# A hybrid layer's attention heads: the samples' scores, log sums and outputs in one PSUM bank, cached keys loaded alone, weights split in quarters, last key tiles in free conv tiles

## The chip, the core and the metric

The kernel runs on one core of a Trainium2 chip. The metric is device time of one execution in microseconds (us): the median of three runs. The engines of the core have short names in the profile: PE is TensorE (matmuls and transposes), PEld its weight loads, ACT ScalarE, DVE VectorE, POOL GpSimd, and SP SyncE, which here only issues DMAs. PSUM, the memory that matmuls write, has eight banks of 512 float columns for each of 128 partitions.

## The reference

One layer of an encoder trunk is computed for 512 prompt frames and 64 sample frames (576 rows, `T`), with a model width of 2048. The 64 sample frames also attend to 512 cached frames.

```python
def stick_breaking(q, k, v, q_pos, k_pos):
    z = jnp.einsum('bqhd,bkhd->bhqk', q, k) / math.sqrt(HEAD_DIM)
    mask = (k_pos[None, :] < q_pos[:, None])[None, None]
    log_1mb = jnp.where(mask, jax.nn.log_sigmoid(-z), 0.0)
    after = lax.cumsum(log_1mb, axis=3, reverse=True) - log_1mb
    w = jnp.where(mask, jnp.exp(jax.nn.log_sigmoid(z) + after), 0.0)
    return jnp.einsum('bhqk,bkhd->bqhd', w, v)

def hybrid_layer(...):
    hn = rmsnorm(x, g_norm1)
    proj = hn @ w_in
    q, k, v, gb, gc, hc = jnp.split(proj, [...], axis=-1)
    ...
    o_attn = stick_breaking_blocks(q, k_all, v_all, P).reshape(B, T, ATTN_W)
    ...
    mix = jnp.concatenate([rmsnorm(o_attn, g_attn_out), rmsnorm(o_conv, g_conv_out)], axis=-1)
    x = x + mix @ w_out
    h2 = rmsnorm(x, g_norm2)
    x = x + (jax.nn.silu(h2 @ w_gate) * (h2 @ w_up)) @ w_down
    return x, k, v, new_conv
```

q and k are normalized per head (8 heads of 128), and `o_conv` is a short gated convolution over gb, gc and hc. New key and value rows and the convolution's state are outputs too.

## The kernel before

All products are made in float32 precision from two fp32r parts of each operand, a rounded high part and the rest: three matmuls (high by high, low by high, high by low) stand for one. ScalarE casts the high part and VectorE subtracts it. Activations lie channel by channel on the partitions with the 576 rows as columns, in two halves of 288 (`HALVES`).

*The input product* (about 0 to 603 us) runs over 22 units of two 128-column groups, each in seven products as in Strassen's scheme. `order` (L898 to L904) lists the pairs (unit, product) in the order in which TensorE runs them; unit -1 is the last, a pair of value heads, and unit -2 the last pair of query and key groups. For a product `run` issues 24 matmuls of 288 columns, and `prepare` four places ahead builds its weight form. `a_done` (L802 on) takes the sums out of PSUM: for values and for queries and keys into tiles `E`, allocated by `e_tile`, which have the tag "e" with two buffers. `normed` normalizes them 17 ticks later and stores them in `qk_dram` (L788); `tokens` transposes the key and value tiles (L749, L758) and stores the rows. For the convolution, tiles `c0` and `c1` of the pool `lpool` are used, whose last conv unit is gb 3 (n = -3). After the product (-1, 3), `xpool` is released and the eight groups of the convolution's result, `mixc`, are loaded from DRAM into its place (L920).

*The first half of the output projection* (603 to 817 us) multiplies `mixc` with eight blocks of 256 columns of w_out (`out_proj`, L978). Each block makes four sums `pjo` (three PSUM banks of the pool `ps_pj`), and each sum takes eight ticks of three matmuls (`product`, L214), 32 ticks for a block. VectorE scales a sum and adds it to the residual tiles `x2t` (L986, L987), which are loaded at the start (L969).

The eight heads run between these ticks. `Pipeline` calls generators when their tick has come: `yield 8` in `attend` means eight ticks later. A new head starts every 29 ticks (`PERIOD`). For TensorE, the order in which the program is written is the order of execution; on ACT, DVE, POOL and SP a scheduler decides it within the dependencies, and each of these queues then runs strictly in order. DMAs take eight semaphores in turn, so that a DMA's issue also waits until the one eight places before it has landed.

In `attend(h)`, the three PSUM banks z2, z1, z0 hold the prompt's scores (L1060), their softplus goes to ScalarE, VectorE and GpSimd, triangular matmuls add the log sums, `weights` (L1116) makes the exponentials, and `po` (L1152 on) sums the outputs. The samples have a path of their own: scores `zs` of 64 queries against four cached key blocks and the new one (L1085 to L1088), log sums `cz` (L1105 to L1109), exponentials in `ws` (L1114), outputs `os` (L1167 to L1170). `keys_cached` transposes the loaded cached keys `cK` on TensorE into `kc` and copies them to `kcT`; it is called eight ticks after zs for the next head (L1102). `kc`, `zs`, `cz`, `po` and `os` all come from `misc`, a tag with two banks used in turn. `load_qk` (L943) loads queries, keys and cached keys of the next head after zs, `load_v` its values at the end of the head. `mixed` (L1145) takes po and os out into the tiles `mixa`, and their squares go through the tiles `sqa` (L1164, L1165, L1172).

The samples' matmuls run on 128 query columns: the last 128 of the rows, of which the last 64 are the samples. The five blocks overlap in the bank at 64-column steps, each overwriting the useless half of the one before.

`next_weight` (L198) hands out the blocks of w_out and the first blocks of the gate and up weights, 20 in all, each 2048 wide per partition. At the start of block i it splits the whole of block i + 1 (two casts and two subtractions of 1024, L179 and L180), and loads block i + 2 (L187).

*The second half of the projection*, on `mixa` (to 917 us), and then the gate, up and down products follow.

Of the kernel before, what the change touches and what calls it, by code (L numbers as in the profile page):

```python
# [10 lines left out]
F32 = mybir.dt.float32  # L11
F32R = mybir.dt.float32r
AF = mybir.ActivationFunctionType
# [3 lines left out]
P = 128  # L17
# [84 lines left out]
def tile_hybrid_stream_step(  # L102
# [95 lines left out]
    def next_weight():  # L198
        i = pos[0]
        pos[0] += 1  # L200
        end = first_block
        while len(raws) < min(i + 2, end):
            load_weight()
        while len(ready) < min(i + 2, end):
            split_weight(nc.vector)
        while len(raws) < min(i + 3, end):
            load_weight()
        out = ready[i]
        ready[i] = None
        return out  # L210
# [591 lines left out]
    def a_done(n, c, i, ps, part):  # L802
        kind, g = UNITS[n][:2]
        a, b = HALVES[i]
        if kind in ("v", "qk"):
            if (n, c) not in etile:
                etile[n, c] = e_tile(f"E{n}")
            E = etile[n, c]
            bank = ps
            if part is not None:  # L810
                nc.vector.tensor_tensor(out=E[:, a:b], in0=ps, in1=part, op=ALU.add)  # L811
# [89 lines left out]
    for n in range(2 - NA, -3):  # L901
        order += [(n + 1, 1), (n, 3), (n, 4), (n + 1, 2), (n + 1, 6), (n + 1, 7), (n + 1, 5)]
    order += [(-2, 1), (-3, 3), (-3, 4), (-2, 2), (-2, 6), (-2, 5), (-2, 3), (-1, 1), (-1, 2), (-1, 3),
              (-2, 7), (-2, 4), (-1, 6), (-1, 5), (-1, 7), (-1, 4)]  # L904
# [25 lines left out]
    ws = bpool.tile([P, 384], F32, name="ws")  # L930
# [12 lines left out]
    def load_qk(h):  # L943
        nc.sync.dma_start(out=qf, in_=qk_dram[h, 0])
        nc.sync.dma_start(out=kf, in_=qk_dram[h, 1])
        nc.sync.dma_start(out=cK, in_=ck[:, h, :].rearrange("(i p) d -> p i d", p=P))
        split(qh, ql, qf[:, :TP])
        split(kh, kl, kf[:, :TP])

    load_qk(0)  # L950
    nc.vector.tensor_scalar(out=neg1r, in0=ident, scalar1=0.0, scalar2=-1.0, op0=ALU.mult, op1=ALU.add)
# [88 lines left out]
    def keys_cached():  # L1040
        kc = misc("kc")
        for i in range(4):
            nc.tensor.transpose(kc[:, i * P : (i + 1) * P], cK[:, i, :], ident)
        nc.scalar.copy(out=kcT, in_=kc)

# [3 lines left out]
    def attend(h):  # L1049
# [12 lines left out]
        for b in (2, 1, 0):  # L1062
# [19 lines left out]
            if h == 0 and b == 1:  # L1082
                keys_cached()

        zs = misc("zs")  # L1085
        for b in (4, 3, 2, 1, 0):
            lk = kf[:, T - P : T] if b == 4 else kcT[:, b * P : (b + 1) * P]
            mm(zs[:, b * TS : b * TS + P], lk, qf[:, T - P : T], start=True, stop=True, skip_group_check=True)  # L1088
        nc.scalar.copy(out=ws[:, TS:], in_=zs[:, TS : TS + 320])
        if h + 1 < NH:  # L1090
            load_qk(h + 1)
        softplus(sp[:, :320], ws[:, TS:], sp[:, :320])
# [8 lines left out]
        if h + 1 < NH:  # L1101
            keys_cached()  # L1102

        def sample_weights():
            cz = misc("cz")  # L1105
            mm(cz[:, :320], trir, sph[:, :320], start=True, stop=False, skip_group_check=True)
            mm(cz[:, :320], trir, spl[:, :320], stop=False, **kw)
            mm(cz[:, :256], neg1r, sph[:, 320:], stop=False, **kw)
            mm(cz[:, :256], neg1r, spl[:, 320:], stop=True, **kw)  # L1109
            nc.gpsimd.memset(ws[:, :TS], 0.0)  # L1110
            nc.vector.tensor_tensor(out=ws[:, TS:], in0=cz[:, :320], in1=ws[:, TS:], op=ALU.add)
# [40 lines left out]
        po = misc("po")  # L1152
# [14 lines left out]
        os_ = misc("os")  # L1167
        for b in range(5):
            lv = vtok[:, 4, :] if b == 4 else cV[:, b, :]
            mm(os_[:, :P], lv, ws[:, b * TS : b * TS + P], start=(b == 0), stop=(b == 4))  # L1170
        mixed(os_[:, TS:P], TP, T)
        nc.scalar.activation(out=sq[1][:, TP - HALF :], in_=os_[:, TS:P], func=AF.Square)  # L1172
# [416 lines left out]
```

## Time and profile before

| | us |
|---|---|
| median of three runs | 2425.6 (2424.18 to 2425.93) |
| the profiled execution's own time | 2424.55 |
| its span in the profile | 2422.8 |
| PE busy in the span | 2357.9 |
| DVE busy | 1938.7 |
| ACT busy | 1235.0 |
| mean granted clock of TensorE | 0.992 |

A row of the waits names the engine, tile and line that waited, what released it, and the total in us, the number of times and the longest. A row of the timeline gives start and length, engine, line, operation, output and inputs, shapes and how many of them were run together; in brackets stands how long the engine had stood idle before and who released it. A row of the engines' busy time in a window gives the window, its length, busy us and instructions of PE, PEld, DVE, ACT and POOL, then the granted clock, the share of the DMA engines' time, and GB/s. A row of the groups has line, engine, operation, tiles, shapes and count, then the sum in us and the mean in ns, then the idle time just before. TensorE's fp32 matmuls appear as two records each.

### The profile page before, as it was taken

To read this page: it belongs to the slowest core of one execution; us is meant where nothing else is said; L and a number is where in the kernel's file an instruction comes from. 1 tells how busy PE (TensorE), PEld (TensorE's weight loads), DVE (VectorE), ACT (ScalarE), POOL (GpSimd) and SP (SyncE) were. 2 spreads that over 40 slices of the span, in tenths; PEclk is the share of its full clock that TensorE was granted. 3 is DMA by queue.
4 is the path that set the end of the run, shared out by engine and by line. 5 is a ranking of instruction groups with operands and counts; after the bars stand their busy time and mean duration, and the time that the engine had idled before them with its cause. 6 is when DMAs were issued, how large, how long until landed. Compare 5 with 4: busy or idle time off the path is not lost.

```text
span 2422.8 us, 43771 instructions
## 1 busy us (share of the span) xinstructions
PE 2357.9 (97%) x17609; PEld 2342.3 (97%) x17609; DVE 1938.7 (80%) x2810; ACT 1235.0 (51%) x2177; POOL 297.9 (12%) x385
## 2 busy tenths in 40 slices
PE   8899999998898999999999999999999899999998
PEld 8899999998888999999999999999999899999998
DVE  7889888796666767888888888888888777877875
ACT  7456656455676545444444444444444444444454
POOL 0111121120132221000000000000000001431211
PEclk9999999999999999999999999999999999999999
DMA  7434343445532233444444435444444935885642
GB/s 259 131 112 122 92 139 94 151 124 181 196 109 79 95 124 103 145 144 149 134 134 149 157 111 160 152 127 146 144 149 129 329 131 187 228 232 194 203 126 79
DMA packets 474899, 360.60 MB, mean 149 GB/s; under 512 B 11278, under 2 KB 460680, under 8 KB 474696
## 3 DMA queue, kind: packets, MB, share of 16 engines
q1 hardware_dynamic: 469528, 351.02, 45.3%
q0 software_dynamic: 5168, 6.79, 1.6%
q8 instruction: 138, 2.26, 0.4%
q14 instruction: 65, 0.53, 0.1%
HBM read 281.39 MB, written 76.37 MB: 148 GB/s over the span
## 4 chain that ended last, share of the span: by engine, by line
PE 84%; DVE 5%; ACT 3%; DMA 2%; issue 2%; POOL 1%; SPq 0%; DVEq 0%; ACTq 0%; POOLq 0%
PE psy L396 43%; PE psw L396 21%; PE psx L396 10%; PE pjo L218 6%; PE pw L1371 2%; DVE whl L223 1%; DVE wlo L180 1%; ACT whl L222 0%; PE pot L1494 0%; DVE c L857 0%; DVE raw_b L340 0%; DMA raw_a<-in_w_down_dram 0%; ACT ph L222 0%; DMA cK<-in_cache_k_dram 0%; DMA out_dram<-tokz 0%
## 5 line engine op out<-in xcount | busy, mean ns | idle before, releaser
L223 DVE TENSOR_TENSOR whl<-raw_a,whl 128x1024 fp32r<-128x1024 f32 (+4 forms) x376 | 425.9, 1133 | 71.7 <-ACT whl L222 70.3
L396 PE MATMUL psy<-t,whl 128*128 128x288 f32 x2916 | 438.0, 295 | 0.5 <-ACT part L419 0.5
L222 ACT CAST whl<-raw_a 128x1024 fp32r<-128x1024 f32 (+4 forms) x376 | 352.1, 937 | 138.9 <-PE psx L396 49.6
L396 PE MATMUL psy<-h_s,whl 128*128 128x288 f32 x2724 | 411.9, 295 | 6.6 <-ACT part L419 6.6
L396 PEld LDWEIGHTS psy<-t,whl 128*128 128x128 f32 x2916 | 403.0, 188 | 0.9 <-ACT part L419 0.7
L396 PEld LDWEIGHTS psy<-h_s,whl 128*128 128x128 f32 x2724 | 378.2, 189 | 7.1 <-ACT part L419 7.1
L396 PE MATMUL psw<-t,whl 128*128 128x288 f32 x2592 | 376.9, 295 | 0.0
L396 PEld LDWEIGHTS psw<-t,whl 128*128 128x128 f32 x2592 | 354.2, 188 | 0.2
L223 DVE TENSOR_TENSOR whl<-raw_b,whl 128x1024 fp32r<-128x1024 f32 (+5 forms) x230 | 249.2, 1084 | 88.9 <-ACT whl L222 87.9
L222 ACT CAST whl<-raw_b 128x1024 fp32r<-128x1024 f32 (+5 forms) x230 | 207.2, 902 | 212.9 <-PE psw L396 76.4
L419 ACT COPY part<-psy 128x288 f32<-128x288 f32 x303 | 121.1, 400 | 353.0 <-PE psy L396 349.7
L396 PE MATMUL psx<-h_s,whl 128*128 128x288 f32 x1122 | 166.3, 296 | 2.5 <-DVE gs L1351 2.5
L396 PEld LDWEIGHTS psx<-h_s,whl 128*128 128x128 f32 x1122 | 155.1, 190 | 2.7 <-issue 2.7
L396 PE MATMUL psw<-t34a,whl 128*128 128x288 f32 x1056 | 152.0, 297 | 5.1 <-DVE E-2_6443 L811 3.7
L222 ACT CAST whl<-s 128x1024 fp32r<-128x1024 f32 (+5 forms) x101 | 93.2, 923 | 118.3 <-PE psw L396 110.1
L396 PE MATMUL psy<-t12a,whl 128*128 128x288 f32 x1056 | 150.1, 295 | 3.1 <-ACT part L419 3.1
L396 PEld LDWEIGHTS psw<-t34a,whl 128*128 128x128 f32 x1056 | 144.8, 190 | 5.8 <-issue 3.9
L396 PEld LDWEIGHTS psy<-t12a,whl 128*128 128x128 f32 x1056 | 143.1, 188 | 4.0 <-ACT part L419 4.0
L218 PE MATMUL pjo<-mixc,whi 128*128 128x288 f32 x512 | 124.1, 309 | 0.0
L223 DVE TENSOR_TENSOR whl<-s,whl 128x1024 fp32r<-128x1024 f32 (+5 forms) x101 | 107.5, 1065 | 19.1 <-ACT whl L222 17.6
L1314 POOL DMA_DIRECT2D hid_dram<-form x3 | 2.4, 807 | 922.4 <-DVE form L223 922.4
L218 PE MATMUL pjo<-mixa,whi 128*128 128x288 f32 x512 | 102.1, 295 | 0.0
(607 smaller groups left out, 4144.8 us busy)
## 6 DMA issues: line engine op xcount, KB each, us to landing
hid_dram<-form SPq DMA_DIRECT2D x147, 288.0 KB, 2.3
raw_a<-in_w_gate_dram SPq DMA_DIRECT2D x23, 1024.0 KB, 6.1
raw_a<-in_w_up_dram SPq DMA_DIRECT2D x23, 1024.0 KB, 6.0
raw_a<-in_w_in_dram SPq DMA_DIRECT2D x22, 1024.0 KB, 5.6
raw_b<-in_w_in_dram SPq DMA_DIRECT2D x22, 1024.0 KB, 7.9
raw_b<-in_w_gate_dram SPq DMA_DIRECT2D x21, 1024.0 KB, 6.6
raw_b<-in_w_up_dram SPq DMA_DIRECT2D x21, 1024.0 KB, 8.2
h_s<-hid_dram SPq DMA_DIRECT2D x10, 2016.0 KB, 10.2
```

The costliest lines, as they stand in the source:

```text
L180: lo_eng.tensor_tensor(out=lo[:, a:b], in0=raw[:, a:b], in1=hi[:, a:b].bitcast(F32), op=ALU.subtract)
L218: mm(ps, w_[:, k, csl], x_[:, a:b], start=(k == 0 and n == 0), stop=(k == nk - 1 and n == 2))
L222: nc.scalar.copy(out=hi, in_=src)
L223: (lo_eng or nc.vector).tensor_tensor(out=lo, in0=src, in1=hi.bitcast(F32), op=ALU.subtract)
L396: mm(ps, whl[:, w_, j, :], x_, start=(start and j == 0 and q == 0), stop=(j == len(xs_) - 1 and q == 2), skip_group_check=True)
L419: nc.scalar.copy(out=t, in_=st["y"])
L1314: q.dma_start(out=hid_dram[fp][2 * n - 2 : 2 * n].rearrange("f p t -> p f t"), in_=t.bitcast(F32))
L1371: mm(pss[j, i], w_[:, k, j * P : (j + 1) * P], x_, start=(kk == 0 and k == 0 and n == 0), stop=(kk == 1 and k == 7 and n == 2))
```

## The change

Five things are done.

1. `next_weight` no longer splits block i + 1 at once: a generator `pieces_of` splits it in four quarters of 512 columns, seven ticks apart. Only a block that is needed at once is split whole.
2. The two `E` tiles of unit -2 are allocated in the conv tiles c0 and c1 of `lpool` instead of the tag "e".
3. The end of `order` changes: (-2,3) goes behind (-1,1), (-1,3) behind (-2,4), so that the release of `xpool` and the loads of `mixc` come two products later.
4. `cK` is loaded by a function of its own, which `keys_cached(h)` calls for head h + 1 right after its transposes; of the `x2t` tiles, two are loaded at the start and one more is written at each block.
5. The samples' scores, log sums and outputs share one `misc` bank: scores run on the 64 sample columns alone, the log sums accumulate onto them in PSUM, the exponential reads PSUM, and os lies in columns 384 to 448. The copy to `ws`, the addition of `cz` and a memset go. `kc` and `po` come from the three banks of `ps_pj`.

```diff
+        def pieces_of(j):
+            hi, lo = weight_split(j)
+            for a in range(0, 2048, 512):
+                weight_parts(raws[j][:, :2048], hi, lo, a, a + 512, nc.vector)
+                yield 7
+
         while len(raws) < min(i + 2, end):
             load_weight()
-        while len(ready) < min(i + 2, end):
+        if len(ready) <= i:
             split_weight(nc.vector)
         while len(raws) < min(i + 3, end):
             load_weight()
+        if i + 1 < end:
+            pipe.spawn(pieces_of(i + 1))
+            pipe.run_due()
...
-                etile[n, c] = e_tile(f"E{n}")
+                etile[n, c] = lpool.tile([P, UW - 2], F32, tag=f"c{c}", name="E2")[:, :T] if n == -2 else e_tile(f"E{n}")
...
-    order += [(-2, 1), (-3, 3), (-3, 4), (-2, 2), (-2, 6), (-2, 5), (-2, 3), (-1, 1), (-1, 2), (-1, 3),
-              (-2, 7), (-2, 4), (-1, 6), (-1, 5), (-1, 7), (-1, 4)]
+    order += [(-2, 1), (-3, 3), (-3, 4), (-2, 2), (-2, 6), (-2, 5), (-1, 1), (-2, 3), (-1, 2), (-2, 7),
+              (-2, 4), (-1, 3), (-1, 6), (-1, 5), (-1, 7), (-1, 4)]
...
-    ws = bpool.tile([P, 384], F32, name="ws")
+    ws = bpool.tile([P, 320], F32, name="ws")
...
     def load_qk(h):
         nc.sync.dma_start(out=qf, in_=qk_dram[h, 0])
         nc.sync.dma_start(out=kf, in_=qk_dram[h, 1])
-        nc.sync.dma_start(out=cK, in_=ck[:, h, :].rearrange("(i p) d -> p i d", p=P))
         split(qh, ql, qf[:, :TP])
         split(kh, kl, kf[:, :TP])
 
+    def load_cached_keys(h):
+        nc.sync.dma_start(out=cK, in_=ck[:, h, :].rearrange("(i p) d -> p i d", p=P))
+
     load_qk(0)
+    load_cached_keys(0)
...
-    for j in range(NP):
-        x2t.append(ypool.tile([P, 2, T], F32, tag=f"y{j}", name=f"x2_{j}"))
-        nc.sync.dma_start(out=x2t[j], in_=xt_dram[2 * j : 2 * j + 2].rearrange("k p t -> p k t"))
+
+    def load_x2():
+        j = len(x2t)
+        if j < NP:
+            x2t.append(ypool.tile([P, 2, T], F32, tag=f"y{j}", name=f"x2_{j}"))
+            nc.sync.dma_start(out=x2t[j], in_=xt_dram[2 * j : 2 * j + 2].rearrange("k p t -> p k t"))
+
+    load_x2()
+    load_x2()
...
             whi, wlo = next_weight()
+            load_x2()
...
-    def keys_cached():
-        kc = misc("kc")
+    def keys_cached(h):
+        kc = ps_pj.tile([P, 512], F32, tag="pj", name="kc")
         for i in range(4):
             nc.tensor.transpose(kc[:, i * P : (i + 1) * P], cK[:, i, :], ident)
         nc.scalar.copy(out=kcT, in_=kc)
+        if h + 1 < NH:
+            load_cached_keys(h + 1)
...
         zs = misc("zs")
-        for b in (4, 3, 2, 1, 0):
+        for n, b in enumerate((4, 3, 2, 1, 0)):
             lk = kf[:, T - P : T] if b == 4 else kcT[:, b * P : (b + 1) * P]
-            mm(zs[:, b * TS : b * TS + P], lk, qf[:, T - P : T], start=True, stop=True, skip_group_check=True)
-        nc.scalar.copy(out=ws[:, TS:], in_=zs[:, TS : TS + 320])
+            mm(zs[:, b * TS : (b + 1) * TS], lk, qf[:, TP:T], start=(n == 0), stop=False, skip_group_check=True)
         if h + 1 < NH:
             load_qk(h + 1)
-        softplus(sp[:, :320], ws[:, TS:], sp[:, :320])
+        softplus(sp[:, :320], zs[:, :320], sp[:, :320])
...
-            cz = misc("cz")
-            mm(cz[:, :320], trir, sph[:, :320], start=True, stop=False, skip_group_check=True)
-            mm(cz[:, :320], trir, spl[:, :320], stop=False, **kw)
-            mm(cz[:, :256], neg1r, sph[:, 320:], stop=False, **kw)
-            mm(cz[:, :256], neg1r, spl[:, 320:], stop=True, **kw)
-            nc.gpsimd.memset(ws[:, :TS], 0.0)
-            nc.vector.tensor_tensor(out=ws[:, TS:], in0=cz[:, :320], in1=ws[:, TS:], op=ALU.add)
-            nc.vector.scalar_tensor_tensor(out=ws[:, 320:], in0=ws[:, 320:], scalar=0.0, in1=sneg,
+            mm(zs[:, :320], trir, sph[:, :320], stop=False, **kw)
+            mm(zs[:, :320], trir, spl[:, :320], stop=False, **kw)
+            mm(zs[:, :256], neg1r, sph[:, 320:], stop=False, **kw)
+            mm(zs[:, :256], neg1r, spl[:, 320:], stop=True, **kw)
+            nc.vector.scalar_tensor_tensor(out=zs[:, 256:320], in0=zs[:, 256:320], scalar=0.0, in1=sneg,
                                            op0=ALU.min, op1=ALU.add)
-            nc.scalar.activation(out=ws[:, TS:], in_=ws[:, TS:], func=AF.Exp)
+            nc.scalar.activation(out=ws, in_=zs[:, :320], func=AF.Exp)
...
-        po = misc("po")
+        po = ps_pj.tile([P, 512], F32, tag="pj", name="po")
...
-        os_ = misc("os")
+        os_ = zs[:, 384 : 384 + TS]
         for b in range(5):
             lv = vtok[:, 4, :] if b == 4 else cV[:, b, :]
-            mm(os_[:, :P], lv, ws[:, b * TS : b * TS + P], start=(b == 0), stop=(b == 4))
-        mixed(os_[:, TS:P], TP, T)
-        nc.scalar.activation(out=sq[1][:, TP - HALF :], in_=os_[:, TS:P], func=AF.Square)
+            mm(os_, lv, ws[:, b * TS : (b + 1) * TS], start=(b == 0), stop=(b == 4), skip_group_check=True)
+        mixed(os_, TP, T)
+        nc.scalar.activation(out=sq[1][:, TP - HALF :], in_=os_, func=AF.Square)
```

More of the change, by code (lines that the diff above doesn't have):

```diff
@@ L1082, in attend @@
             if h == 0 and b == 1:
-                keys_cached()
+                keys_cached(0)
         zs = misc("zs")
-        for b in (4, 3, 2, 1, 0):
+        for n, b in enumerate((4, 3, 2, 1, 0)):
             lk = kf[:, T - P : T] if b == 4 else kcT[:, b * P : (b + 1) * P]
-            mm(zs[:, b * TS : b * TS + P], lk, qf[:, T - P : T], start=True, stop=True, skip_group_check=True)
-        nc.scalar.copy(out=ws[:, TS:], in_=zs[:, TS : TS + 320])
+            mm(zs[:, b * TS : (b + 1) * TS], lk, qf[:, TP:T], start=(n == 0), stop=False, skip_group_check=True)
         if h + 1 < NH:
             load_qk(h + 1)
-        softplus(sp[:, :320], ws[:, TS:], sp[:, :320])
+        softplus(sp[:, :320], zs[:, :320], sp[:, :320])
         nc.gpsimd.tensor_tensor(out=sp[:, 256:320], in0=sp[:, 256:320], in1=s01, op=ALU.mult)
@@ L1101, in attend @@
         if h + 1 < NH:
-            keys_cached()
+            keys_cached(h + 1)
         def sample_weights():
-            cz = misc("cz")
-            mm(cz[:, :320], trir, sph[:, :320], start=True, stop=False, skip_group_check=True)
-            mm(cz[:, :320], trir, spl[:, :320], stop=False, **kw)
-            mm(cz[:, :256], neg1r, sph[:, 320:], stop=False, **kw)
-            mm(cz[:, :256], neg1r, spl[:, 320:], stop=True, **kw)
-            nc.gpsimd.memset(ws[:, :TS], 0.0)
-            nc.vector.tensor_tensor(out=ws[:, TS:], in0=cz[:, :320], in1=ws[:, TS:], op=ALU.add)
-            nc.vector.scalar_tensor_tensor(out=ws[:, 320:], in0=ws[:, 320:], scalar=0.0, in1=sneg,
+            mm(zs[:, :320], trir, sph[:, :320], stop=False, **kw)
[3 more added lines that the diff above has]
+            nc.vector.scalar_tensor_tensor(out=zs[:, 256:320], in0=zs[:, 256:320], scalar=0.0, in1=sneg,
                                            op0=ALU.min, op1=ALU.add)
-            nc.scalar.activation(out=ws[:, TS:], in_=ws[:, TS:], func=AF.Exp)
+            nc.scalar.activation(out=ws, in_=zs[:, :320], func=AF.Exp)
         def weights(b):
```

## The prediction

> **What bounds the kernel now.** I read the busy table, the shares of the chain that ended last, TensorE's waits around the stages that the diff touches, the engines' busy time there, and then the timeline at each stall.
>
> ```profile
> PE 2357.9 (97%) x17609; PEld 2342.3 (97%) x17609; DVE 1938.7 (80%) x2810; ACT 1235.0 (51%) x2177; POOL 297.9 (12%) x385
> PE 84%; DVE 5%; ACT 3%; DMA 2%; issue 2%; POOL 1%; SPq 0%; DVEq 0%; ACTq 0%; POOLq 0%
> 640.00:812.00 172.00, 156.62 (x1098) 150.98 (x1097) 118.84 (x243) 122.02 (x269) 48.41 (x99) 0.97 0.30 95
> 820.00:960.00 140.00, 140.00 (x1058) 140.00 (x1058) 99.70 (x170) 69.65 (x128) 35.36 (x38) 1.00 0.33 112
> ```
>
> TensorE is the bound, 97% busy and 84% of the chain. The change removes no matmul of the large products, so it can only win where TensorE stands still, runs at a lower clock, or does the heads' small matmuls. The columns of the last two rows are PE, PEld, DVE, ACT, POOL, granted clock, DMA share and GB/s: the attention heads (640 to 812) leave TensorE 15 us idle, and from 820 there is nothing to gain. TensorE's waits between 595 and 822 us show where it stands:
>
> ```profile
> PE zs L1088 <- ACT sqa L1165: 10.8, 5, 3.8
> PE kc L1043 <- DMA cK<-in_cache_k_dram: 5.9, 1, 5.9
> PE zs L1088 <- DVE pl L223: 3.5, 2, 2.0
> PE ssg L276 <- ACT tok L751: 1.4, 1, 1.4
> ```
>
> Seven of the eight heads stall at the samples' scores zs, 14.3 us together. One cached-key transpose stalls 5.9 us on its load. The change touches both.
>
> **A. The end of the input product** (new order, E-2 in the conv tiles).
>
> ```profile
> 581.06 4.72 PE L396 MATMUL psw<-t34a,whl 128*128 128x288 f32 x24 [3.69 <-DVE E-2_6443 L811]
> 585.61 3.34 PE L396 MATMUL psy<-t12a,whl 128*128 128x288 f32 x24
> 589.44 1.06 PE L396 MATMUL psy<-t12a,whl 128*128 128x288 f32 x6 [0.49 <-ACT part L419]
> 600.22 0.63 PE L749 MATMUL tok_a<-ident,E-2_6443 128*128 128x128 f32 x4 [1.17 <-DVE E-2_6443 L784]
> 575.70 5.00 SPq L920 DMA_DIRECT2D mixc<-mixc_dram  x8
> ```
>
> E-2_6443 took the "e" buffer of E-2_6187, so its first sum waited until that tile had gone to qk_dram, and TensorE with it: 3.69 us. With a buffer of its own this goes. The 24 matmuls after it took 4.72 instead of 3.34 us (half-speed pitch after the stall): 1.38 more. The 0.49 stands between products whose order changes; I count it as gone at best. Against this: the new order brings products that add into the same E-2 tiles nearer together ((-2,3) stood four places ahead of (-2,7) and stands two ahead now), and a sum may be asked for before VectorE has read the one before it; the nearest row is the 0.49 itself, so +0.5. The tok_a wait of 1.17 stays. The ssg wait of 1.4 comes from ScalarE's copies of the last token tiles, which move closer to it: between 0 and +2, taken +0.5. The mixc loads leave with (-1,3), two products later. A product of 24 matmuls lasts 3.34 us, so they leave near 582.4 instead of 575.70, and their issue alone takes 5.00, to 587.4. The last transposes of stage A at 600.22 come some 5 us earlier, and the first product on mixc behind them near 597: 9.6 us after the last issue, which I take as just in time. Sum: -3.69 - 1.38 - 0.49 + 0.5 + 0.5 = -4.6, rounded to -5. Ends: -2 (half the stall comes back as a wait for mixc or tok) and -6.5 (no new wait, ssg's own 0.9 shorter).
>
> **B. Cached keys loaded alone.**
>
> ```profile
> 614.76 0.60 PE L1043 MATMUL kc<-ident,cK 128*128 128x128 f32 x4
> 617.67 0.45 SPq L1035 DMA_DIRECT2D vtok<-v_dram  x1
> 622.86 0.38 SPq L946 DMA_DIRECT2D cK<-in_cache_k_dram  x1
> 626.59 1.09 PE L1043 MATMUL kc<-ident,cK 128*128 128x128 f32 x4 [5.85 <-DMA cK<-in_cache_k_dram]
> 626.00:632.00 6.00, 5.41 (x25) 5.44 (x26) 3.23 (x6) 4.62 (x12) 1.57 (x3) 0.53 0.68 205
> ```
>
> Head 0 is done with cK at 615.4, but the next load is written behind zs, and on SP's queue it follows vtok, cV, qf and kf, so it leaves at 622.86 and TensorE waits for it at 620.7 to 626.6. Now it is written right behind the transpose. It needs 3.7 us from issue to use, so an issue before 617 suffices; the transpose ends at 615.4. SP is then busy with the last stores of stage A, which may hold it for a few us (each load also waits for the DMA eight before it on its semaphore). Gone at best: 5.85 plus the clock after it, at most 6 x (1 - 0.53) = 2.8. Bounds 0 and -8.65; I take -7, because the load needs only to come 5.85 earlier, which its four predecessors on the queue alone (617.67 to 622.86) nearly are. For x2 only two tiles load up front; the rest are wanted later, one pair of rows per block, and TensorE waits for none of them: 0.
>
> **C. The heads.** Timeline at each zs, and the clock around the longer ones:
>
> ```profile
> 648.38 0.49 PE L1088 MATMUL zs<-qf,kf 128*128 128x128 f32 x2 [1.48 <-ACT sqa L1165]
> 671.18 0.49 PE L1088 MATMUL zs<-qf,kf 128*128 128x128 f32 x2 [2.12 <-ACT sqa L1165]
> 744.00 0.53 PE L1088 MATMUL zs<-qf,kf 128*128 128x128 f32 x2 [3.80 <-ACT sqa L1165]
> 768.51 0.49 PE L1088 MATMUL zs<-qf,kf 128*128 128x128 f32 x2 [2.19 <-ACT sqa L1165]
> 670.00:676.00 6.00, 4.82 (x26) 4.82 (x27) 3.46 (x8) 4.87 (x15) 2.31 (x4) 0.72 0.60 191
> 694.00:700.00 6.00, 4.40 (x23) 4.41 (x24) 2.75 (x7) 4.81 (x14) 2.14 (x4) 0.72 0.65 196
> 742.00:748.00 6.00, 4.00 (x20) 4.00 (x20) 3.59 (x8) 4.99 (x14) 2.91 (x5) 0.72 0.96 291
> 767.00:773.00 6.00, 4.49 (x35) 4.49 (x36) 5.39 (x8) 4.21 (x13) 3.74 (x5) 1.00 0.80 257
> ```
>
> zs, kc, cz, po and os shared two banks in turn, so a head's zs needed the bank of the head before's po, whose squares (sqa) and split ScalarE and VectorE read late. Now kc and po come from the out projection's three banks, and zs, the log sums and os share one: zs waits for nobody of the head before. What waited there passes on: kc, eight ticks after zs, comes next, but the longest stall was 3.80, and zs itself with eight ticks of three matmuls (the x24 row) lasts 1.3 + 3.3 = 4.6, so its bank is free. Gone at best: 14.3, plus the clock in three windows, 3 x 6 x (1 - 0.72) = 5.0.
>
> [...]
>
> Scores and outputs go from 128 columns to 64:
>
> ```profile
> L1088 PE MATMUL zs<-qf,kcT 128*128 128x128 f32 x64 | 9.6, 299 | 0.0
> L1170 PE MATMUL os<-ws,cV 128*128 128x128 f32 x64 | 8.5, 276 | 0.0
> 14.03 0.46 PE L541 MATMUL psx_s<-ident,xsn 64*128 64x64 f32 x4
> ```
>
> With the last key block these are 5/4 of 128 records, 160. No 64-column record with 128 rows is there; the nearest, four of 64 columns on 64 rows, take 0.46, against 0.60 for four of 128 (the kc row above): 0.035 each, 160 x 0.035 = 5.6. Bounds 0 and half of the 9.6 + 8.5 us, 9; taken 5.
>
> [...]
>
> So at most 14.3 + 5.0 + 5 = 24. But the heads are not TensorE's alone:
>
> ```profile
> ACT sph L222 <- POOL hbl L1097: 16.2, 6, 3.4
> ACT pr L1120 <- DVE z L1118: 12.7, 10, 1.8
> DVE pl L223 <- ACT ph L222: 14.7, 18, 1.6
> L1089 ACT COPY ws<-zs 128x320 f32<-128x320 f32 x8 | 3.4, 420 | 0.3 <-PE zs L1088 0.3
> L1111 DVE TENSOR_TENSOR ws<-cz,ws 128x320 f32<-128x320 f32 x8 | 3.9, 484 | 0.0
> L179 ACT CAST whi<-raw_a 128x1024 fp32r<-128x1024 f32 x40 | 40.5, 1045 | 14.2 <-PE pjo L218 9.5 <-PE pw L1371 4.0 <-PE psw L396 0.6
> L222 ACT CAST qh<-qf 128x512 fp32r<-128x512 f32 x8 | 4.9, 610 | 0.0
> ```
>
> In these 172 us ScalarE works 122 and waits 29 more on VectorE and GpSimd in these two groups alone, and VectorE works 119 and waits 15 on ScalarE in one group. The three feed each other, and from 671.18 to 768.51 four heads take 24.3 us each. A zs that starts at once only helps as far as this mesh keeps up. It loses work per head: the copy of zs (0.42) and the addition to cz (0.48), 0.9 x 7 = 6.3. It gains the cut of weights into quarters: four casts of 512 for a weight are 4 x 0.61 against 2 x 1.045, +0.35, and with about 7 weights in the stage +2.4 (VectorE's part I leave in its waits). So the mesh alone shortens by about 3 to 4, and that is the lower end (-3). Smaller pieces also delay a head's operation by half as long. Between -3 and -24 I take the middle, -14, because the releaser at five zs was the po of the head before, which goes, and at two the mesh itself (pl).
>
> The quarters cost nothing elsewhere: from 820 on ScalarE is busy 70 of 140 us. If that cover were gone they would cost 12 more weights x 0.35 = 4.
>
> **Sum.** -5 - 7 - 14 = -26. The profiled execution took 2424.55 us (span 2422.8), 1.05 under the median, so about 2399.6: **2400**.
>
> **Rivals.**
>
> *All of it is gained.* A -6.5, B -8.65, C -24 and the whole of the narrow records (9 for 5): -43, so **2382**. For it: zs waits only for the po bank. Against: the mesh above.
>
> *The mesh paces the heads.* Period stays near 24 us, TensorE's waits move from zs to po, z or the log sums, and the narrow records only lengthen them: A -5, B -7, C -3, so -15, **2411**. For it: ScalarE's busy time and waits fill 151 of 172 us. Against: those waits include some that come from TensorE's own lateness.
>
> *Hidden anyway* (the change doesn't do what it says). cK leaves no earlier, since SP is still at stage A's stores; zs's wait reappears at kc or pjo, which now share three banks. A -2, B 0, C -3: **2420**.
>
> *Slower: SP's queue.*
>
> ```profile
> SPq L187 <- DVE wlo L180: 26.1, 3, 16.1
> SPq L1036 <- PE os L1170: 55.7, 6, 19.5
> 638.27 0.37 SPq L187 DMA_DIRECT2D raw_a<-in_w_out_dram  x1
> 661.99 0.38 SPq L187 DMA_DIRECT2D raw_a<-in_w_out_dram  x1
> ```
>
> A weight load on SP waits for the last subtraction of the weight two before it; SP stood 16.1 us at one. That subtraction is now the fourth quarter, 21 of a block's 32 ticks in, and qf, kf, cK, cV and vtok of the next head stand behind the load. If they come late, each head stalls as kc did, 5.85 + 2.8 = 8.65; from three heads on this eats the 26 (3 x 8.65), and with five it is -26 + 43 = +17: **2442**. Against it: weight loads come once in 24 us, with 11 ticks left after the last quarter, and cK now leaves earlier in the head.
>
> **How the numbers follow.** Forecast 0.47, all gained 0.13, mesh 0.24, hidden 0.07, slower 0.09. A difference under 0.2%, 4.9 us, can't be told from none; that is 2420.7 to 2430.5. The hidden case lies at that border and is split, 0.04 to the same and 0.03 to faster; a part of the slower case with few late heads, 0.01, is also the same. So faster 0.87, same 0.05, slower 0.08. The forecast's own range, with half the way to each bound, is 2392 to 2409. For eight in ten it reaches over the mesh case to 2419 and down into the full gain to 2385, which leaves out about half of that case, the hidden and the slower one: 0.2.
>
> **What would show it.** A: no wait on E-2_6443 in TensorE's waits and the last input product ending some 5 us earlier; a wait for mixc or tok above 2 us refutes it. B: cK's second load issued by 617 and no wait at the second kc. C: no wait of zs on sqa, head period near 22 us, granted clock near 1.00 in the windows; zs records of 64 columns shorter. If instead po, pjo or the log sums wait on ACT or DVE with the period still at 24, the mesh rival holds; if qf, kf or cK loads appear as releasers in several heads, the slower one. No change after 820 is expected; a difference there would mean that I missed a part.

## The result, and the profile after

| | before | changed |
|---|---|---|
| median on the same chip, us | 2424.89 (2423.67 to 2425.93, 4 runs) | 2407.68 (2405.93 to 2413.04, 4 runs) |
| ratio | | 0.993, 95% interval 0.9918 to 0.9942 |
| span of the profiled execution, us | 2422.8 | 2406.8 |
| mean granted clock | 0.992 | 0.994 |

The kernel is 17.2 us faster where 26 had been forecast. TensorE is busy for nearly the same time (2355.5 us against 2357.9), and its idle time is smaller (51.3 us against 64.9). First the busy line of the page and TensorE's largest waits from 550 to 822 us in the changed kernel (line numbers are 9 to 21 higher than before), then its engines' busy time in three windows, in the columns used above.

```profile
PE 2355.5 (98%) x17609; PEld 2339.5 (97%) x17609; DVE 1939.7 (81%) x2840; ACT 1235.0 (51%) x2207; POOL 298.9 (12%) x377
```

```profile
PE po L1170 <- ACT pr L1137: 5.3, 4, 2.5
PE z L1147 <- ACT ph L231: 2.5, 1, 2.5
PE ssg L286 <- DVE s2g L232: 1.7, 1, 1.7
PE pjo L227 <- ACT kcT L1063: 1.2, 1, 1.2
PE ssg L285 <- ACT tok L760: 0.7, 1, 0.7
PE psw L405 <- DVE E L820: 0.6, 1, 0.6
PE ssg L285 <- ACT s2g L231: 0.6, 1, 0.6
```

```profile
603.00:640.00 37.00, 33.55 (x219) 32.06 (x219) 23.87 (x53) 24.47 (x54) 7.40 (x15) 0.91 0.86 289
640.00:812.00 172.00, 163.50 (x1155) 157.13 (x1154) 124.18 (x266) 121.65 (x279) 48.23 (x89) 0.98 0.30 97
820.00:960.00 140.00, 140.00 (x1059) 140.00 (x1058) 102.51 (x186) 69.16 (x140) 34.46 (x38) 1.00 0.38 125
```

No zs or kc stands among the waits any more, and of the 3.69 us for the last key tile (E-2 before, E now) 0.6 are left. In their place TensorE waits for ScalarE's exponentials at po (5.3), for the first head's z (2.5) and at the group scale's ssg (3.0 in three waits, where it was 1.4). In the heads it is now busy 163.5 of 172 us instead of 156.6. From 820 on nothing changed.

Where the time came from is read off four marks in the two timelines: the last stall before the stage that the diff touches, and the scores zs of heads 0, 1 and 7. Before:

```profile
556.68 3.47 PE L396 MATMUL psy<-t12a,whl 128*128 128x288 f32 x24 [1.63 <-ACT part L419]
616.28 0.38 PE L1088 MATMUL zs<-qf,kf 128*128 128x128 f32 x2
791.96 0.49 PE L1088 MATMUL zs<-qf,kf 128*128 128x128 f32 x2 [1.24 <-ACT sqa L1165]
```

Changed:

```profile
557.78 3.47 PE L405 MATMUL psy<-t12a,whl 128*128 128x288 f32 x24 [1.63 <-ACT part L428]
614.60 0.33 PE L1109 MATMUL zs<-qf,kf 128*128 128x64 f32 x2
639.80 0.33 PE L1109 MATMUL zs<-qf,kf 128*128 128x64 f32 x2
775.21 0.33 PE L1109 MATMUL zs<-qf,kf 128*128 128x64 f32 x2
```

| stretch | before | changed | difference |
|---|---|---|---|
| start to the mark at 557 | 556.7 | 557.8 | +1.1 |
| mark to zs of head 0 | 59.6 | 56.8 | -2.8 |
| zs of head 0 to zs of head 1 (648.38 before) | 32.1 | 25.2 | -6.9 |
| zs of head 1 to zs of head 7 | 143.6 | 135.4 | -8.2 |
| zs of head 7 to the end of the span | 1630.8 | 1631.6 | +0.8 |

They add up to the 16.0 us between the spans. The first row moved by as much in runs whose edit lies behind it (556.1 to 558.6 over the runs). The second takes 59.2 to 62.0 us in the six profiles, of before and of the experiments below, that have neither the new order nor the quarters, so that a single profile tells no term finer than about 3 us. The profile of before lies at the low end of these; five profiles with the new order have 54.8 to 57.7, and the means, 60.9 and 56.6, are 4.2 us apart. Read by this table, part A brought 2.8 (forecast 5), B 6.9 (7) and C 8.2 (14). The experiments show that this reading is wrong for B and C.

### The profile page after: what moved, and what is told of

Its sections match the earlier page's. It is cut to its first block, busy times and chain, and to the rows that moved or that the text cites. A ratio compares the mean times of both kernels' runs of the same rounds, so it can differ in the third digit from the quotient of the medians.

```text
span 2406.8 us, 43812 instructions
## 1 busy us (share of the span) xinstructions
PE 2355.5 (98%) x17609; PEld 2339.5 (97%) x17609; DVE 1939.7 (81%) x2840; ACT 1235.0 (51%) x2207; POOL 298.9 (12%) x377
## 4 chain that ended last, share of the span: by engine, by line
PE 82%; DVE 6%; ACT 4%; issue 2%; POOL 2%; DMA 1%; SPq 0%; ACTq 0%; DVEq 0%; POOLq 0%
PE psy L405 43%; PE psw L405 21%; PE psx L405 10%; PE pjo L227 5%; DVE whl L232 1%; ACT whl L231 1%; PE pw L1388 1%; ACT ph L231 0%; PE psv L405 0%; PE pot L1511 0%; DVE c L866 0%; DVE raw_b L349 0%; POOL hbl L1117 0%; DMA raw_a<-in_w_down_dram 0%; DVE wlo L180 0%
```

## The experiments

Each ratio is against runs of the kernel before on the same chip.

| run | median, us | ratio | 95% interval |
|---|---|---|---|
| own_key_load | 2423.67 | 0.9994 | 0.9985 to 1.0003 |
| other_banks | 2425.17 | 1.0000 | 0.9990 to 1.0010 |
| late_key_tiles | 2425.10 | 0.9997 | 0.9988 to 1.0007 |
| quarters_alone | 2425.84 | 1.0005 | 0.9995 to 1.0014 |
| key_load_and_x2 | 2421.33 | 0.9986 | 0.9977 to 0.9996 |
| key_x2_and_order | 2418.44 | 0.9971 | 0.9960 to 0.9982 |
| heads_alone | 2412.45 | 0.9945 | 0.9930 to 0.9960 |
| all_but_quarters | 2405.66 | 0.9920 | 0.9905 to 0.9935 |
| merged_with_copies | 2410.00 | 0.9932 | 0.9917 to 0.9947 |
| exp_twice | 2410.36 | 0.9933 | 0.9916 to 0.9949 |
| later_scale | 2405.28 | 0.9912 | 0.9898 to 0.9927 |
| later_scale_and_po | 2519.60 | 1.0384 | 1.0369 to 1.0400 |

The medians of before were 2425.64 in the first four runs, 2424.77 in the next four and 2427.44 in the last four.

### One part at a time

**own_key_load**: the kernel before, with this alone.

```diff
-        nc.sync.dma_start(out=cK, in_=ck[:, h, :]...)      # in load_qk
+    def load_cached_keys(h):
+        nc.sync.dma_start(out=cK, in_=ck[:, h, :]...)
...
         nc.scalar.copy(out=kcT, in_=kc)
+        if h + 1 < NH:
+            load_cached_keys(h + 1)
```

> Before, with only the load of the cached keys written right behind their transpose. Forecast's theory: the wait of 5.85 us at the second kc and the slow clock behind it go, zs(0) to zs(1) falls from 32.1 us to about 25 as in the changed kernel, the kernel is 6 to 8 us faster, and the zs stalls of heads 2 to 7 stay at 13 us. Rival (SP is held anyway, and the gain in the changed kernel came from its other parts): second cK issued no earlier than 620, 0 to -2 us.

The rival held. These rows are from its timeline of SP (start, length, line, DMA and how many of them):

```profile
603.83 5.97 SPq L972 DMA_DIRECT2D x<-xt_dram  x7
624.11 0.38 SPq L950 DMA_DIRECT2D cK<-in_cache_k_dram  x1
```

and this one is from TensorE's:

```profile
627.11 1.09 PE L1046 MATMUL kc<-ident,cK 128*128 128x128 f32 x4 [5.32 <-DMA cK<-in_cache_k_dram]
```

The load did move ahead of qf and kf, but it left at 624.11, no earlier than before (622.86). What stands further ahead on SP are seven residual tiles x2, 6 us of issue, and behind them the token stores, of which the first took 4.86 us to issue (610.73). Whether they hold it is tested below with x2 moved.

**late_key_tiles**: only the last key tiles in the conv tiles, and the new order.

```diff
-                etile[n, c] = e_tile(f"E{n}")
+                etile[n, c] = lpool.tile([P, UW - 2], F32, tag=f"c{c}", name="E2")[:, :T] if n == -2 else e_tile(f"E{n}")
...
-    ... (-2, 5), (-2, 3), (-1, 1), (-1, 2), (-1, 3), (-2, 7), (-2, 4), (-1, 6), ...
+    ... (-2, 5), (-1, 1), (-2, 3), (-1, 2), (-2, 7), (-2, 4), (-1, 3), (-1, 6), ...
```

> Before, with only the last key tiles in the conv tiles and the new order at the end of the input product. Forecast's theory: the 3.69 us wait and 1.4 us of slow clock go, little comes back, zs(0) comes 4 to 5 us earlier, the kernel is 4 to 5 us faster. Rival (the wait passes on to the group scale's matmuls ssg whatever the weights do): zs(0) earlier by under 2 us as in the changed kernel (1.7), ssg waits of 2 us or more.

The zs of head 0 came at 613.07 instead of 616.28, though the mark stood 1.6 us later (558.23): 4.8 us gained up to there, as forecast. And the kernel was not faster: by its time the theory failed, and the ssg waits of 2.4 us that the rival named were there too. Its timeline of TensorE shows where it went, and that of SP why:

```profile
603.23 0.40 PE L277 MATMUL ssg<-s2g,oner 128*128 128x288 f32 x1 [1.58 <-DVE s2g L223]
629.22 1.09 PE L1043 MATMUL kc<-ident,cK 128*128 128x128 f32 x4 [11.70 <-DMA cK<-in_cache_k_dram]
```

```profile
603.55 5.96 SPq L969 DMA_DIRECT2D x<-xt_dram  x8
624.23 0.42 SPq L946 DMA_DIRECT2D cK<-in_cache_k_dram  x1
```

TensorE came earlier to a load that came no earlier. The wait of 3.7 us left the input product and came back, with interest, in the wait for cK: 11.70 instead of 5.85.

**other_banks**: only kc and po in the out projection's banks.

```diff
-        kc = misc("kc")
+        kc = ps_pj.tile([P, 512], F32, tag="pj", name="kc")
...
-        po = misc("po")
+        po = ps_pj.tile([P, 512], F32, tag="pj", name="po")
```

> Before, with only kc and po moved to the out projection's banks; zs, cz and os keep two banks in turn and their 128 columns. Forecast's theory (mesh gives a part back): no wait of zs on sqa, but new waits at po, z or kc of 5 us or more in sum; zs(1) to zs(7) falls from 143.6 us to 135 to 139, the kernel is 4 to 9 us faster. Rival A (TensorE alone paces): zs(1) to zs(7) near 126, 14 us or more faster. Rival B (the merge of the samples' banks made the gain in the heads, not the moved banks): 0 to -2 us.

No zs waited any more, and zs of head 1 to zs of head 7 took 140.1 instead of 143.6. The waits of TensorE from 640 to 812, and a piece of VectorE's and of TensorE's timeline, show what took their place:

```profile
PE po L1153 <- ACT pr L1120: 6.3, 5, 2.6
PE pjo L218 <- DVE x L987: 5.8, 3, 2.1
PE pjo L218 <- ACT kcT L1044: 1.3, 1, 1.3
```

```profile
676.15 0.56 DVE L223 TENSOR_TENSOR s0l<-hbl,s0h 128x384 fp32r<-128x384 f32 x1 [2.36 <-ACT s0h L222]
...
677.48 0.46 DVE L986 TENSOR_TENSOR pjo<-pjo,Rc 128x288 f32<-128x288 f32 x1
677.97 0.46 DVE L987 TENSOR_TENSOR x<-pjo,x 128x288 f32<-128x288 f32 x1
```

```profile
678.49 0.41 PE L218 MATMUL pjo<-mixc,whi 128*128 128x288 f32 x1 [1.89 <-DVE x L987]
```

With kc and po in them, the three banks no longer cover VectorE's delay. VectorE stood 2.36 us for ScalarE at s0l; the scaling and the addition of a finished sum were queued behind that, and the next pjo waited 1.89 us for its bank. With po's 6.3 the 14.3 us of before came back almost whole. Rival B held.

**quarters_alone**: only the weights in quarters (the first block of the diff above).

> Before, with only the weights split in quarters. Forecast's theory: hidden, within 1 us of before. Rival (the quarters of block 1 run on ScalarE and VectorE ahead of the group scale's casts, and TensorE waits at ssg, as the changed kernel shows with 3.0 us there): zs(0) later by 2 to 4 us, heads unchanged, the kernel 2 to 4 us slower.

The ratio says no change. The profile shows the rival's place: ssg waited 2.19 us for ScalarE instead of 1.44 (up to 1.93 in the others with the old order), and zs of head 0 came 63.4 us behind the mark, where the six profiles named above have 59.2 to 62.0. From zs of head 1 to that of head 7 it took 146.1 us instead of 143.6, but from there to the end of the span 2.6 us less. So neither expectation fits the stages: time moved between them, and the medians show none lost.

So these four edits, each alone, brought 2.0, 0.5, 0.5 and -0.2 us against 2425.64: together under 3 us, of the 17 that the whole brings. Two edits of the whole are not among them, the spreading of x2 and the one bank on 64 columns. They were run only together with others, so that it is not known what either brings by itself.

### Parts together

**key_load_and_x2**: own_key_load, and x2 loaded two tiles at the start and one per block.

```diff
-    for j in range(NP):
-        x2t.append(...); nc.sync.dma_start(out=x2t[j], ...)
+    load_x2()
+    load_x2()
...
             whi, wlo = next_weight()
+            load_x2()
```

> Before, with the own load of the cached keys and the residual tiles x2 loaded two at the start and one per block. Theory (SP's queue: the seven x2 loads in a row, 5 to 6 us of issue and 12 us of transfers at 400 GB/s, held cK back in the run with the key load alone): second cK issued before 618, the wait of 5.9 us at the second kc and the slow clock behind it gone, zs(0) to zs(1) near 25 us, 5 to 8 us faster. Rival (the key load is late for another reason, such as the token stores ahead of it): the wait at kc stays above 4 us, 0 to -2 us.

In the trace the theory of SP's queue held. Its SP timeline:

```profile
616.98 0.38 SPq L950 DMA_DIRECT2D cK<-in_cache_k_dram  x1
623.25 2.36 SPq L975 DMA_DIRECT2D x<-xt_dram  x4
```

cK now leaves at 616.98, 7 us earlier than with its own load alone, four x2 tiles follow 6 us later, the first of the last token stores takes 0.38 us to issue instead of 4.86, and the second kc waits for nothing. From zs of head 0 to that of head 1 it took 25.3 us instead of 32.1. Of these 6.8 us, 4.6 are left in the span (2418.2) and 3.4 in the medians (interval 1.0 to 5.6), less than the 5 expected: in the profile zs of head 0 came at 617.89, 1.6 us later than before, within the spread given above. The own load alone had 2.0 in the medians, and the two intervals overlap; that x2 spread is worth time is seen in the trace and not clear of noise in the medians.

**key_x2_and_order**: the same with late_key_tiles.

> As the run with key load and x2, and also the last key tiles in the conv tiles with the new order. Theory (alone, the earlier end of the input product only made TensorE wait 11.7 instead of 5.9 us for the same cK): now its 3 to 5 us are kept, 8 to 12 us faster than before. Rival (the ssg waits and the next late load eat it): no more than 1.5 us better than the run without the order.

Now the earlier end of the input product keeps 2.9 us (2418.44 against 2421.33), between theory and rival; the two intervals overlap. Its timeline shows the rest:

```profile
602.70 0.40 PE L277 MATMUL ssg<-s2g,oner 128*128 128x288 f32 x1 [1.57 <-DVE s2g L223]
619.58 0.63 PE L1053 MATMUL kc<-ident,cK 128*128 128x128 f32 x4 [1.12 <-DMA cK<-in_cache_k_dram]
625.01 0.44 PE L1142 MATMUL z<-ph,trir 128*128 128x384 f32 x1 [1.34 <-ACT ph L222]
```

TensorE comes earlier to the group scale, to cK and to head 0's chain, and each is a little late in turn.

**heads_alone**: the whole of the samples' part (scores, log sums and outputs in one bank on 64 columns, kc and po in the other banks), the rest as before.

> Before, with the whole of the samples' part: one bank for scores, log sums and outputs on 64 columns, kc and po in the out projection's banks; key load, x2, order and weights as before. Theory (with the moved banks alone the wait passed on to pjo, 1.9 us four times for the residual addition on VectorE; the merge takes 0.9 us per head off ScalarE and VectorE and its one bank never waits): zs(1) to zs(7) near 135 as in the changed kernel, 4 to 8 us faster. Rival (the pjo waits stay, since VectorE's whole-block weight subtractions hold up the residual addition, and only quarters cure it): zs(1) to zs(7) 139 or more, 0 to -3 us.

12.3 us faster, more than the theory had said, though kc still waited 5.12 us for cK. From zs of head 1 to that of head 7 it took 134.5 us instead of 143.6, and from head 0 to head 1 28.9 instead of 32.1. That is the stretch which the table above gives to B, where key_load_and_x2 alone has 25.3 and the whole 25.2: the two parts overlap there, and the table's 8.2 leaves out what C brings in it. TensorE's waits from 640 to 812 against those of other_banks:

```profile
PE po L1149 <- ACT pr L1116: 4.9, 4, 1.8
PE pjo L218 <- ACT kcT L1044: 1.9, 2, 1.2
...
PE pjo L218 <- DVE x L987: 0.3, 1, 0.3
```

The pjo waits for VectorE are down from 5.8 to 0.3. At the place shown above, VectorE now runs in this order:

```profile
669.82 0.47 DVE L986 TENSOR_TENSOR pjo<-pjo,Rc 128x288 f32<-128x288 f32 x1 [1.21 <-PE pjo L218]
670.98 0.56 DVE L223 TENSOR_TENSOR s0l<-hbl,s0h 128x384 fp32r<-128x384 f32 x1 [0.70 <-ACT s0h L222]
...
672.31 0.45 DVE L987 TENSOR_TENSOR x<-pjo,x 128x288 f32<-128x288 f32 x1
```

The scheduler has put the scaling ahead of s0l, whose own wait is 0.70 instead of 2.36.

**merged_with_copies** asks whether the dropped work pays, or the bank.

```diff
+        nc.scalar.copy(out=ws, in_=zs[:, :320])
-        softplus(sp[:, :320], zs[:, :320], sp[:, :320])
+        softplus(sp[:, :320], ws, sp[:, :320])
...
+            nc.vector.tensor_scalar(out=ws, in0=zs[:, :320], scalar1=0.0, scalar2=None, op0=ALU.add)
-            nc.vector.scalar_tensor_tensor(out=zs[:, 256:320], in0=zs[:, 256:320], ...)
+            nc.vector.scalar_tensor_tensor(out=ws[:, 256:320], in0=ws[:, 256:320], ...)
-            nc.scalar.activation(out=ws, in_=zs[:, :320], func=AF.Exp)
+            nc.scalar.activation(out=ws, in_=ws, func=AF.Exp)
```

> The run with the heads alone (2412.45), but with the two operations that the merge had dropped put back on the merged bank: ScalarE copies the scores to ws before the softplus, and VectorE copies the log sums to ws before the exponential. Theory (the merge pays because it takes 0.9 us of chained ScalarE and VectorE work off each head): most of its 12 us is lost, 2420 to 2425, with pjo waiting for VectorE or po for ScalarE again. Rival (it pays because one bank serves the samples, whatever the work): within 3 us of 2412.

The rival held: nothing is lost (2410.00, ratio 0.9932, against 2412.45 and 0.9945). Its engines' busy time from 640 to 812, and TensorE's largest wait there:

```profile
640.00:812.00 172.00, 165.61 (x1189) 159.03 (x1190) 127.24 (x267) 128.16 (x282) 47.73 (x93) 1.00 0.32 102
```

```profile
PE po L1151 <- ACT pr L1118: 3.5, 3, 1.7
```

ScalarE is busy 128 instead of 122 us, VectorE 127 instead of 121, and TensorE waits less than without the copies. So the gain of the merge is not the work that it takes off ScalarE and VectorE; GpSimd's memset, 0.15 us a head, was not put back. What is left are the one bank and the order that the scheduler makes of the program with it; no run tells these two apart, and none has the one bank with kc and po left in their old banks.

**all_but_quarters**: the changed kernel with the weights split at once in two pieces.

> The changed kernel with the weights split at once in two pieces of 1024 as before. Theory (forecast: quarters are hidden): within 2 us of the changed kernel, 2405 to 2410. Rival (they matter once the banks are shared: VectorE's 2.4 us of subtractions in a row delay the residual addition and pjo waits for it): pjo <- DVE waits of 1 us and more in several heads, 3 to 8 us slower than the changed kernel.

2405.66 against 2407.68: the quarters bring nothing, and may cost 2 us; the intervals (0.9905 to 0.9935, 0.9918 to 0.9942) overlap, and no long wait of pjo for VectorE appeared without them. This total, 19.1 us, is close to the sum of the heads' 12.3 and the 6.3 of key_x2_and_order, 18.6.

### What paces the heads

**exp_twice**: the changed kernel, with a line written twice.

```diff
             nc.scalar.activation(out=pr[b][:, : full[b]], in_=z[b][:, : full[b]], func=AF.Exp)
+            nc.scalar.activation(out=pr[b][:, : full[b]], in_=z[b][:, : full[b]], func=AF.Exp)
```

> The changed kernel (2407.7) with each of the three exponentials of a head's prompt weights written twice in a row, 0.5 us each, so 1.5 us more of ScalarE per head in the middle of the chain, 12 us in eight heads; results are the same. Theory (ScalarE, VectorE and GpSimd pace the heads): 8 us or more slower, the period of 22.6 us near 24. Rival (TensorE paces, 95% busy from 640 to 812): under 3 us slower.

The ratio stays (0.9933 against 0.9930); the medians differ by 2.7 us. Its engines' busy time and TensorE's largest wait from 640 to 812:

```profile
640.00:812.00 172.00, 163.12 (x1139) 157.17 (x1138) 122.44 (x261) 129.08 (x298) 49.38 (x91) 0.96 0.31 96
```

```profile
PE po L1171 <- ACT pr L1138: 7.6, 5, 3.0
```

ScalarE is busy 129.1 instead of 121.7 us there, 7.4 more in the middle of the chain. The wait at po grew from 5.3 to 7.6, and zs of head 1 to that of head 7 from 135.4 to 137.7; the rest vanished in time in which ScalarE had stood. ScalarE's load does not pace the heads.

**later_scale** and **later_scale_and_po**: all_but_quarters with these delays.

```diff
-        yield 4
+        yield 6          # group_scale, both runs
...
-        yield 2
+        yield 4          # ahead of po, second run only
```

> The kernel without quarters (2405.66) with the group scale's matmuls ssg six instead of four ticks after their casts, so that they ask later for s2g. Theory (the ssg waits at 600 to 605 of 1.6 and 0.7 us are a matter of the place only): they shrink below 1 us in sum and the kernel is 1 to 3 us faster. Rival (the time passes on to the wait of z for ph at 626, since the heads' first chain starts no earlier): within 1 us.

> As later_scale, and the first matmul of po four instead of two ticks after the last exponential. Theory (po's waits for ScalarE, 5 to 6 us over the heads, are a matter of two ticks of about 0.4 us each): they fall by 0.8 us each where they are that long, 2 to 4 us faster than later_scale. Rival (the head grows by two ticks, the next head's softplus then waits for po to free its weights, and os and zs come nearer together): same or slower.

By its median the first is within 1 us of all_but_quarters (2405.28 against 2405.66), but their runs of before differ (2427.44 and 2424.77): by ratio it is 2 us better (0.9912 against 0.9920), with intervals that overlap. So it decides nothing between theory and rival. The ssg waits shrank only from 2.4 to 1.9 us. The time did not pass on to z, whose wait for ph fell from 2.34 to 0.70; TensorE waited 2.1 us for cK instead, as its timeline shows:

```profile
603.01 0.40 PE L277 MATMUL ssg<-s2g,oner 128*128 128x288 f32 x1 [1.20 <-DVE s2g L223]
620.17 0.63 PE L1053 MATMUL kc<-ident,cK 128*128 128x128 f32 x4 [2.10 <-DMA cK<-in_cache_k_dram]
```

The second was a bad choice. The delays ahead of po add up to 28 ticks (3, 3, 1, 8, 3, 4, 4, 2) and a head starts after 29. With 30, the next head's first scores and softplus are written ahead of po in the program, so po takes the next head's masked softplus for part of its weights and waits for it. The program no longer computes the layer and its time tells nothing on two ticks as such. TensorE's waits from 600 to 812:

```profile
PE po L1164 <- ACT ph L222: 31.6, 10, 3.8
PE po L1161 <- POOL pr L1085: 20.3, 5, 6.3
```

## Why the forecast of 26 us came out as 17

By the medians of the parts A brought 2.9 of its 5 us, B with the x2 loads 3.4 of 7, C 12.3 of 14, and the quarters, forecast at 0, cost about 2, which isn't clear of noise: 16.6 in all, close to the 17.2 of the whole. Most of the missing 9 us stands in A and B.

**A, the end of the input product (forecast -5).** The steps on the buffer were right: the 3.69 us wait and the slow matmuls behind it are gone (24 took 4.72 us at a granted clock of 0.50 from 581 to 583; the unbroken products of 24 from 553 to 598 take 3.33 to 3.48 now), and alone the part brought zs of head 0 4.8 us forward. What failed is the closing of the account at the end of the stage. The forecast asked what is late next at mixc, tok and ssg, not whether the next transfer (cK) comes earlier too. And its +0.5 for ssg was too small: in the changed kernel the last matmuls of the input product end at 598.3 us instead of 603.4, the 5 us that were forecast, but TensorE then waits 3.0 us at ssg instead of 1.4, and its granted clock from 606 to 612 is 0.76 where it was 1.00. It was below 0.93 there in five of the seven profiles with the new order, and 0.96 to 1.00 in the seven with the old. Alone the gain is 0.5 us; with the load put right it is 2.9.

**B, the cached keys (forecast -7).** The number fits the stretch (zs of head 0 to zs of head 1: -6.9), but for the wrong reason, and in the time of the kernel about half of it is left. The forecast took the load's place in the program for its place in time, with vtok, cV, qf and kf as what held it, and priced the x2 edit at "0". The own load alone brought 2.0, which is not distinct from nothing, and its cK left no earlier. With x2 spread over the blocks it left 7 us earlier. By the trace the edit that was costed at nothing is what lets the other one act; of the two together 3.4 us are left in the medians, 4.6 in the span. Whether x2 spread would do without the own load was not run.

**C, the heads (forecast -14).** The heads' part alone brought 12.3. The size is close, but three terms under it were wrong, so that part of the agreement is luck. First, the 64 columns were to give 5 us and gave none: both timelines show ten records of scores, before

```profile
648.38 0.49 PE L1088 MATMUL zs<-qf,kf 128*128 128x128 f32 x2 [1.48 <-ACT sqa L1165]
648.71 1.06 PE L1088 MATMUL zs<-qf,kcT 128*128 128x128 f32 x8
649.52 0.38 PE L218 MATMUL pjo<-mixc,whi 128*128 128x288 f32 x1
```

and changed

```profile
639.80 0.33 PE L1109 MATMUL zs<-qf,kf 128*128 128x64 f32 x2
639.96 1.06 PE L1109 MATMUL zs<-qf,kcT 128*128 128x64 f32 x8
640.83 0.38 PE L227 MATMUL pjo<-mixc,whi 128*128 128x288 f32 x1
```

From the first of the eight to the pjo behind them it is 0.81 us at 128 columns and 0.87 at 64: about 0.1 us a record for both. With all ten it is 1.04 us at 128 columns where no zs waited (other_banks, 670.91 to 671.95) and 1.03 at 64, and ten records of os take 1.03 in both. The forecast read the saving from the lengths in the rows, which overlap from record to record (one of the eight lasts 0.275 us in both kernels); by the distance to the next row the psx_s row shows next to none, 0.39 us for its four beside 0.41 for the four of 128 columns behind it (timeline of before):

```profile
14.42 0.66 PE L544 MATMUL psx<-ident,xin 128*128 128x128 f32 x4
14.83 0.38 PE L661 MATMUL pj<-bod,whi 128*128 128x288 f32 x1
```

The records of the eight weight loads (PEld) last 0.19 us in both kernels (median of L1088 before and L1109 changed) and overlap as well. That the weight load is what sets the distance of 0.1 us is not shown by a run.

Second, the forecast held back 10 of 24 us because ScalarE, VectorE and GpSimd would pace the heads, and priced the merge by the work that it drops, 0.9 us a head. exp_twice and merged_with_copies show that ScalarE has room for 6 to 7 us more, and VectorE for as much in the second, at under 3 us of time; GpSimd was not loaded. The waits that are left suggest why the gain stops at 12: TensorE asks at fixed ticks for something that one chain delivers a little late, po for the exponentials two ticks after they are asked for, pjo for kcT. That would be latency and not load, which the sum of an engine's busy and waiting time doesn't tell apart; no run shows it, since the one with a later po computes something else. The slow clock gave back less than the 5.0 us at best: from 640 to 812 the granted clock went from 0.97 to 0.98, which is about 2 us.

Third, the forecast said that zs then waits for nobody and that what passes on finds a free bank. With kc and po moved and the samples' banks as they were, zs was free, but the wait came back at pjo and po (other_banks: no gain). It ended with the merge.

**Quarters (forecast 0).** Alone +0.2 us, in the whole about +2; neither is clear of noise.

The rival of the mesh gave 2411 and lay nearer to the result than the forecast, but by luck: its period of 24 us fell to 22.6 (135.4 over six heads), and the load of ScalarE and VectorE does not set the pace. The rival "hidden anyway" missed the whole, but it describes two of the parts alone: cK left no earlier (own_key_load), and zs's wait came back at pjo (other_banks). The slower rival, SP's queue, did not come true as it was told: no transfer stands among TensorE's waits from 640 to 812. But its engine was the right one to look at, for B and for A.

What is open: which of the one bank and the scheduler's order makes the merge worth 12 us more than the moved banks; what x2 spread and the one bank bring by themselves; what ends the gain in the heads; and whether the quarters cost 2 us.

## What to carry to other kernels

A wait that is removed can come back at the next thing that is late, so follow the path until it meets something that has itself become earlier: here the earlier end of the input product brought 0.5 us alone and 2.9 with the load put right, and the moved banks brought 0.5 alone and 12.3 with the samples' bank. A load can be held by what stands ahead of it on its queue (cK left at 624.11, and at 616.98 with x2 spread), so price an edit that thins the queue by what stands behind it, not by who waits for its own transfer. Before an engine is called the pace of a stage, load it: an operation written twice, as in exp_twice (7.4 us more of ScalarE, 2.7 us of time), tells room from none in one run.

## What the runs showed of the hardware

With 128 rows and 128 columns of the stationary side, fp32 records with 64 and with 128 moving columns came at the same distance, about 0.1 us (ten in 1.03 us in the changed kernel and in 1.04 us in other_banks).

Seven loads of 576 KB in a row took 4.92 us (before) and 5.97 us (own_key_load) of SP's time to issue, and a token store behind them 4.36 and 4.86 us; with the loads spread such a store took 0.38 us, and a load of 256 KB further back left 7 us earlier (own_key_load and key_load_and_x2).
